# A queue model places TensorE's dependent steps, row maxima move within a unit's fill, long reciprocals go in quarters

## The chip, the cores and the metric

The kernel runs on one core of one Trainium2 chip. The metric is the device time of one execution in microseconds (us); the figure of a kernel is the median of its runs. Each engine of the core works through its own queue in order: TensorE (PE, with the weight loads as PEld), VectorE (DVE), ScalarE (ACT), GpSimd (POOL) and SyncE (SP), which issues the DMAs. An instruction that waits holds up everything behind it on its engine.

## The reference

Two layers (DEPTH 2) over 2048 frames of width 1024, in float32. A layer projects its input into four head groups of four heads each, with a SiLU gate per group, and ends in an output projection and a LayerNorm:

```python
ya = _banded_chunk_attention(aq, ak, av, A_PREV_CHUNKS, rel_bias=rel_bias)      # own chunk + 8 before
yb = _mla(bcq, bckv, bkr, positions, mla_q_norm, w_uq, mla_kv_norm, w_ukv)      # dense chunk-causal
yc = _banded_chunk_attention(qc, kc, cv, SWA_PREV_CHUNKS, sinks=swa_sinks)      # own chunk + 2 before
ym = _memory_attention(mq, mem, w_mem_kv)                                       # 256 memory tokens
gated = jnp.concatenate([ya * jax.nn.silu(ag), yb * jax.nn.silu(bg),
                         yc * jax.nn.silu(cg), ym * jax.nn.silu(mg)], axis=-1)
return _layer_norm(alpha * x + gated @ w_out, ln_gain, ln_bias)
```

All four are softmax attentions: scores, the row's maximum, exp, and the product with v. The kernel holds its operands as pairs (a rounded high part and the rest, `hi` and `lo`), so a product takes three matmuls.

## The kernel before, in words

A layer has three stages. The first computes groups C, M and A for four blocks of 512 frames, six units per block in the order C, M, A, C, M, A, each unit two heads. The second runs group B (`unit_b`, eight units of two heads, with growing numbers of keys). The third (`phase3`) is the output projection with the LayerNorm.

A unit hands `drive` two lists. Its *banks* are score tiles of 512 columns: `do_s` issues the score matmuls (`sc`) and two exps on ACT (`ph` and `p`, lines 478 and 480), `do_l` the difference `pl` on DVE or POOL (498), `do_pv` the product with v (`pv`). `do_s` runs two banks ahead of `do_pv` (LA = 2). Its *fill* is everything that must be done before its banks: projections (`pp`, eight steps of three matmuls), transposes of v (`put_v`: `vf` by ACT, then `pvt` on PE, 400), splits of q and k, and the *row maxima*. `drive` spreads the fill of unit j+1 over the banks of unit j in proportion to written costs; `final`, the fill of the third stage, goes over the last unit.

Row maxima (`maxes`): a matmul writes scores of 128 queries to a PSUM tile `mx` (there are two, shared with `pt`, `pst`, `ptr` and `ptab`), DVE reduces it into a column of `mcol` (449: an add and a maximum, with a read of the accumulator behind it; 880 in M and 1011 in B: a plain maximum). In C a `tensor_scalar` with the sink follows (725), in A and B a small reduction over key blocks (604, 1017). Then `max_row` transposes `mcol` on PE (`pt`, 440), ACT negates it into `mr` (442) and an SP DMA (443) writes the row under the queries, where the head's first `sc` matmul reads it.

The Tile framework sets the order on each engine from the order in which the code is written. The code defers steps with `Clock`: `now` counts TensorE time alone (columns over 2400 per us), and `later(dt, f)` runs `f` when that clock has passed `now + dt`. Before the change these delays are constants:

```python
        later(1.3, tr)       # put_v: pvt after vf
        later(1.0, f)        # max_row: pt after the last maximum
        later(1.2, stats)    # latent: pst after sf
        later(2.5, fin)      # latent_fin
```

If `do_s` reaches a head whose maximum row has not been emitted, `ck.until` emits deferred steps until it has.

Of the kernel before, what the change touches and what calls it, by code (L numbers as in the profile page):

```python
# [16 lines left out]
OP = mybir.AluOpType  # L17
# [76 lines left out]
class Clock:  # L94


    def __init__(self):
        self.now = 0.0
        self.heap = []
        self.n = 0  # L100

# [33 lines left out]
def hybrid(ctx, tc, x, mem, positions, w_in, rel_bias, q_norm, w_uq, kv_norm, w_ukv,  # L135
# [7 lines left out]
    act = nc.scalar.activation  # L143
    dma = nc.sync.dma_start
    tt = nc.vector.tensor_tensor
    stt = nc.vector.scalar_tensor_tensor
    ptt = nc.gpsimd.tensor_tensor
    ck = Clock()
    later = ck.later

# [242 lines left out]
    def put_v(p, vt, t0, n):  # L393
# [11 lines left out]
        later(1.3, tr)  # L405
# [19 lines left out]
    def gate_end(ge, dst):  # L425
# [4 lines left out]
        for z in range(4):  # L430
            def part(c=slice(128 * z, 128 * z + 128)):
                nc.vector.reciprocal(e[:, c], e[:, c])  # L432
                ptt(g[:, c], g[:, c], e[:, c], op=OP.mult)  # L433
# [3 lines left out]
    def max_row(mc, q2t, row, st, i):  # L437
# [119 lines left out]
    def unit_a(l, b, p, D):  # L557
# [24 lines left out]
        def maxes(i):  # L582
# [9 lines left out]
            def one(n):  # L592
                def f():
# [7 lines left out]
                    if n == len(pieces) - 1:  # L601
                        if b:
                            mc = mcol(4)
                            nc.vector.reduce_max(mc, st["mc2", i], axis=AX.X)
# [19 lines left out]
        fill += mix(rest, maxes(0) + maxes(1))  # L624
# [29 lines left out]
        return fill, banks  # L654
# [24 lines left out]
    def unit_c(l, b, p, D):  # L679
# [92 lines left out]
        return fill, banks  # L772

    def latent(l, b, k, p, D):
# [32 lines left out]
        later(1.2, stats)  # L807

    def latent_fin(l, b, D):
# [43 lines left out]
        later(2.5, fin)  # L853

    def unit_m(l, b, p, D):
# [10 lines left out]
        def maxes(i):  # L866
# [3 lines left out]
            def one(n):  # L870
                def f():
# [8 lines left out]
                    nc.vector.reduce_max(st["mc", i][:, 2 * n:2 * n + 2], m.rearrange("p (t k) -> p t k", t=2), axis=AX.X)  # L880
# [7 lines left out]
        fill += pg[:2] + mix(pg[2:], maxes(0) + maxes(1))  # L888
# [11 lines left out]
        return fill, banks  # L900
# [3 lines left out]
    def unit_b(l, b, p, D):  # L904
# [91 lines left out]
        def maxes(i):  # L996
# [3 lines left out]
            def one(n):  # L1000
                def f():
# [8 lines left out]
                    if j < b:  # L1010
                        nc.vector.reduce_max(acc, m, axis=AX.X)  # L1011
                    else:
                        ttr(m, mmask[:, 512 - w:512], acc)
                    if n == len(pieces) - 1:
                        if b:
                            mc = mcol(4)
                            nc.vector.reduce_max(mc, st["mc", i][:, :, 0:b + 1], axis=AX.X)
# [7 lines left out]
            + up([2], 128 * p, kdone) + up([2], 256 + 128 * p, lambda pv: put_v(pv, vpart(b), 0, 4)) \  # L1025
            + maxes(0) + maxes(1)
# [17 lines left out]
        return fill, banks  # L1044
# [6 lines left out]
    def drive(units, final):  # L1051
# [191 lines left out]
    def g_split(D, b, f):  # L1243
# [16 lines left out]
        return ld, sp  # L1260

    def g_prep(D, b):
        pr = [g_split(D, b, f) for f in range(8)]
        steps = []
        for f in range(8):
            def s(f=f):
# [203 lines left out]
```

## Time and profile before

| | us |
|---|---|
| median of 3 runs (lowest, highest) | 2663.76 (2657.4, 2665.67) |
| the profiled execution | 2667.25 |
| its span, first to last instruction | 2665.5 |
| PE busy | 2527.8 |
| DVE busy | 1877.9 |
| ACT busy | 1264.0 |
| POOL busy | 1070.4 |

PE is busy for 95% of the span, so 137.7 us are gaps in front of a matmul. A matmul's listed duration is its latency: neighbours overlap, and the pace is read from the distance between starts.

### The profile page before, as it was taken

The page shows a single profiled execution, that of the slowest core. Times are in us where ns is not written, and L with a number is a line of the kernel's source. Part 1 is how long each engine was busy: PE and PEld are TensorE (multiplying, and loading weights), DVE is VectorE, ACT ScalarE, POOL GpSimd, SP SyncE. Part 2 cuts the span into 40 slices and gives each one's busy share as a digit, 9 for nine tenths or more (in the row PEclk, how much of TensorE's full clock was granted, in tenths as well). Part 3 has the DMA queues.
Part 4 walks back from the last instruction along what each step waited for, and adds up shares of the span by engine and source line. Part 5 has one row for each costly group of instructions (what it writes and reads, how often), then busy time and mean ns, then how long its engine had stood idle before and what let it go on. Part 6 is the DMA issues. An engine that isn't in the chain of part 4 may idle for free.

```text
span 2665.5 us, 36469 instructions
## 1 busy us (share of the span) xinstructions
PE 2527.8 (95%) x12312; PEld 2080.7 (78%) x12312; DVE 1877.9 (70%) x3293; ACT 1264.0 (47%) x2255; POOL 1070.4 (40%) x835
## 2 busy tenths in 40 slices
PE   7899999998999899989999999999999999999998
PEld 6777777887878787768877788788788787877786
DVE  4767768658666876988766566566566578688786
ACT  4545455455444566650024444454544455767200
POOL 4343334343333344453343434434333433445343
PEclk9999999999999999989999999999999999999999
DMA  6545345345335423254345443443443454232432
GB/s 209 165 154 166 110 135 169 102 131 163 115 124 164 149 76 100 64 170 138 135 137 161 147 144 120 131 139 116 134 139 110 144 157 129 63 118 83 147 121 87
DMA packets 176443, 350.91 MB, mean 132 GB/s; under 512 B 25688, under 2 KB 48944, under 8 KB 176256
## 3 DMA queue, kind: packets, MB, share of 16 engines
q1 hardware_dynamic: 176256, 348.58, 42.0%
q8 instruction: 98, 1.61, 0.3%
q14 instruction: 89, 0.73, 0.1%
HBM read 247.43 MB, written 68.02 MB: 118 GB/s over the span
## 4 chain that ended last, share of the span: by engine, by line
PE 33%; DVE 9%; issue 8%; POOL 5%; ACT 3%; DMA 2%; SPq 0%; POOLq 0%; DVEq 0%; ACTq 0%
PE pp L305 15%; PE pv L305 6%; PE sc L305 5%; PE po L305 2%; PE mx L305 2%; DVE pl L498 1%; POOL xr L1344 1%; POOL xr L1343 1%; PE up L305 1%; POOL pl L498 1%; DVE mx L449 1%; DVE xr L1341 1%; ACT p L480 1%; DVE mcol L1011 1%; POOL rs L1337 1%
## 5 line engine op out<-in xcount | busy, mean ns | idle before, releaser
L293 POOL TENSOR_TENSOR wlo<-raw,whi 128x1024 fp32r<-128x1024 f32 x184 | 447.0, 2430 | 656.7 <-ACT whi L288 612.9
L305 PE MATMUL pp<-xh,whi 128*128 128x512 f32 x1472 | 593.6, 403 | 1.5 <-ACT e L415 1.4
L305 PE MATMUL pp<-xl,whi 128*128 128x512 f32 x1472 | 584.6, 397 | 2.5 <-DVE xl L353 1.3
L305 PE MATMUL pp<-xh,wlo 128*128 128x512 f32 x1472 | 583.7, 397 | 1.7 <-POOL wlo L293 1.7
L478 ACT ACTIVATE ph<-sc 128x512 fp32r<-128x512 f32 (+2 forms) x560 | 324.5, 580 | 422.5 <-PE sc L305 399.8
L305 PE MATMUL sc<-Y 96*128 96x512 f32 (+15 forms) x1840 | 466.3, 351 | 3.0 <-ACT p L480 1.5
L498 DVE TENSOR_TENSOR pl<-p,ph 128x512 fp32r<-128x512 f32 (+2 forms) x389 | 316.9, 817 | 186.5 <-ACT p L480 184.0
L305 PE MATMUL pv<-ph,Y 128*128 128x512 f32 (+3 forms) x1520 | 398.5, 343 | 7.9 <-DVE e L423 4.6
L288 ACT ACTIVATE whi<-raw 128x1024 fp32r<-128x1024 f32 x192 | 203.4, 1059 | 336.0 <-issue 131.9
L498 POOL TENSOR_TENSOR pl<-p,ph 128x512 fp32r<-128x512 f32 (+1 forms) x171 | 222.7, 1303 | 341.8 <-ACT p L480 268.8
L305 PEld LDWEIGHTS sc<-Y 96*128 96x128 f32 (+6 forms) x1840 | 317.7, 193 | 43.6 <-ACT p L480 2.9
L305 PEld LDWEIGHTS pp<-xh,wlo 128*128 128x128 f32 x1472 | 280.3, 190 | 63.1 <-POOL wlo L293 2.6
L305 PEld LDWEIGHTS pp<-xh,whi 128*128 128x128 f32 x1472 | 281.4, 191 | 57.5 <-ACT e L415 2.5
L480 ACT ACTIVATE p<-sc 128x512 f32<-128x512 f32 (+2 forms) x560 | 322.8, 576 | 3.1 <-POOL pl L498 3.0
L305 PEld LDWEIGHTS pp<-xl,whi 128*128 128x128 f32 x1472 | 281.1, 191 | 48.7 <-DVE xl L376 2.4
L305 PEld LDWEIGHTS pv<-ph,Y 128*128 128x128 f32 x1520 | 273.8, 193 | 46.1 <-issue 5.3
L305 PE MATMUL pv<-pl,Y 128*128 128x512 f32 (+3 forms) x760 | 265.6, 349 | 20.9 <-DVE pl L498 13.3
L305 PE MATMUL mx<-Y 128*128 128x256 f32 (+6 forms) x800 | 251.8, 340 | 19.5 <-DVE mcol L449 10.9
L449 DVE CUSTOM_DVE_ANT_0 mx<-mx,bts 128x128 f32<-128x128 f32 (+3 forms) x352 | 171.7, 494 | 78.9 <-PE mx L305 69.6
L305 PEld LDWEIGHTS mx<-Y 128*128 128x128 f32 (+1 forms) x800 | 151.8, 193 | 71.0 <-DVE mcol L449 24.3
L433 POOL TENSOR_TENSOR g<-g,e 128x128 f32<-128x128 f32 x192 | 116.1, 613 | 202.0 <-DVE e L432 188.7
L305 PEld LDWEIGHTS pv<-pl,Y 128*128 128x128 f32 x760 | 146.7, 193 | 50.4 <-DVE pl L498 23.6
(249 smaller groups left out, 3620.4 us busy)
## 6 DMA issues: line engine op xcount, KB each, us to landing
raw<-in_w_in_dram SPq DMA_DIRECT2D x184, 512.0 KB
Y<-Y SPq DMA_DIRECT2D x144, 128.0 KB
gr<-gT SPq DMA_DIRECT2D x64, 256.0 KB
gT<-g SPq DMA_DIRECT2D x48, 256.0 KB
cts<-sin SPq DMA_DIRECT2D x40, 256.0 KB
cts<-cos SPq DMA_DIRECT2D x40, 256.0 KB
xt<-in_xT_dram SPq DMA_DIRECT2D x32, 256.0 KB
raw<-in_w_out_dram SPq DMA_DIRECT2D x16, 512.0 KB
```

What stands on the lines that cost most here:

```text
L288: act(hi, raw, AF.Copy)
L293: ptt(lo, raw, f32(hi), op=OP.subtract)
L305: mm(o, lhs, rhs, start=start, stop=stop)
L433: ptt(g[:, c], g[:, c], e[:, c], op=OP.mult)
L449: nc.vector.tensor_tensor_reduce(m, m, table, op0=OP.add, op1=OP.max, scale=1.0, scalar=-3e38, accum_out=acc)
L478: act(bk["ph"][:, :width], sc[:, :width], AF.Exp, scale=scale)
L480: act(bk["p"][:, :width], sc[:, :width], AF.Exp, scale=scale)
L498: (ptt if on_pool else tt)(bk["pl"][:, :w], bk["p"][:, :w], f32(bk["ph"])[:, :w], op=OP.subtract)
L1011: nc.vector.reduce_max(acc, m, axis=AX.X)
L1337: ptt(rs, rs, mhalf[:, 0:1], op=OP.pow)
L1341: nc.vector.tensor_scalar(y[hf], y[hf], mv[:, 0:1], rs, op0=OP.subtract, op1=OP.mult)
L1343: eng(y[hf], y[hf], lgt[hf], op=OP.mult)
```

## The change: what it does, and the diff

`Clock` gets two tables: `free` (when each of DVE, ACT and POOL has finished what it was given) and `made` (when a tensor at an offset is written). Wrappers around the usual instructions (`act`, `tt`, `stt`, `ptt`, `rmax`, `recip`, `ttr`) enter a written cost. `after(ap, dt, f)` runs `f` when the clock has passed the moment at which `ap` is made plus `dt`. It replaces `later` for `pvt`, `pt` and `pst`; `latent_fin` waits 3.5 instead of 2.5. Not entered are `tensor_scalar`, `tensor_copy` and DMAs.

The row maxima move: in A and B the second head's become a third list, `late`, which `drive` spreads over the first half of the unit's own banks; in A the first head's are mixed into all but the last three projection steps; in C and M the last three or two projection steps stand behind all maxima; in B the first head's stand before the projection of v. The reciprocals over 128x512 for the third stage (1256) become four over 128x128, each a step of its own with a cost of 0.3.

```diff
 class Clock:
+    @staticmethod
+    def key(ap):
+        return ap.tensor.name, ap.offset
+
+    def use(self, eng, cost, out, *ins):
+        t = max([self.free.get(eng, 0.0), self.now] + [self.made.get(self.key(a), 0.0) for a in ins if hasattr(a, "tensor")])
+        self.free[eng] = t + cost
+        self.made[self.key(out)] = t + cost + 0.1
+
+    def ready(self, ap):
+        return max(self.now, self.made.get(self.key(ap), 0.0))
...
+    def tt(out, a, b, **kw):
+        ck.use("dve", 0.16 + 0.00115 * cols(out), out, a, b)
+        return nc.vector.tensor_tensor(out, a, b, **kw)
...
+    def after(ap, dt, fn):
+        later(ck.ready(ap) - ck.now + dt, fn)
...
-        later(1.3, tr)
+        after(vf, 0.1, tr)
...
-        later(1.0, f)
+        after(mc, 0.1, f)
...
     def ttr(m, table, acc):
+        ck.use("dve", 0.28 + 0.00108 * cols(m), acc, m)
...
-        fill += mix(rest, maxes(0) + maxes(1))
+        fill += mix(rest[:-3], maxes(0)) + rest[-3:]
+        late = maxes(1)
...
-        if p == 0:
-            fill = fill[:-2] + mix(fill[-2:], late)
-        else:
-            fill = fill[:-8] + mix(fill[-8:], late)
+        fill = fill[:-8] + mix(fill[-8:-3], late) + fill[-3:]
...
-        later(1.2, stats)
+        after(sf, 0.1, stats)
...
-        later(2.5, fin)
+        later(3.5, fin)
...
-        fill += pg[:2] + mix(pg[2:], maxes(0) + maxes(1))
+        fill += pg[:2] + mix(pg[2:6], maxes(0) + maxes(1)) + pg[6:]
...
-            + up([2], 128 * p, kdone) + up([2], 256 + 128 * p, lambda pv: put_v(pv, vpart(b), 0, 4)) \
-            + maxes(0) + maxes(1)
+            + up([2], 128 * p, kdone) + maxes(0) + up([2], 256 + 128 * p, lambda pv: put_v(pv, vpart(b), 0, 4))
+        late = maxes(1)
...
+        for j, u in enumerate(units):
+            if u[2]:
+                a = max(0, marks[j] - LA - 1)
+                jobs.append((a, max(a + 1, marks[j] + len(u[1]) // 2 - LA - 2), u[2]))
...
-        def sp():
+        def sp(z):
+            if f in (2, 3):
+                c = slice(128 * z, 128 * z + 128)
+                recip(st["d"][:, c], st["d"][:, c])
+                if z < 3:
+                    return
+                ptt(st["g"], st["g"], st["d"], op=OP.mult)
             hi, lo = gtile(b, f)
-            if f in (2, 3):
-                nc.vector.reciprocal(st["d"], st["d"])
-                ptt(st["g"], st["g"], st["d"], op=OP.mult)
...
-            steps.append((0.0, s))
+                steps.append((0.3, s))
```

Three places show how the order moves. The first is on PE, in the second M unit of the third block of layer 0: the end of its first head's maxima and their transpose `pt`. Before:

```order
L305 MATMUL mx<-Y 128x256 x2
L305 MATMUL pv<-ph,Y 128x128 x2
L305 MATMUL pv<-pl,Y 128x128
L305 MATMUL pv<-ph,Y 128x384 x2
L305 MATMUL pv<-pl,Y 128x384
L305 MATMUL sc<-Y 128x256 x4
L440 MATMUL pt<-identr,mcol 4x128
L305 MATMUL pp<-xh,whi_81 128x512
```

and now, where the same `pt` follows two steps of the next projection:

```order
L350 MATMUL pv<-ph,Y 128x256 x2
L350 MATMUL pv<-pl,Y 128x256
L350 MATMUL sc<-Y 128x256 x2
L350 MATMUL sc<-Y 128x128 x4
L350 MATMUL pp<-xh,whi_83 128x512
L350 MATMUL pp<-xl,whi_83 128x512
L350 MATMUL pp<-xh,wlo_84 128x512
L350 MATMUL pp<-xh,whi_83 128x512
L350 MATMUL pp<-xl,whi_83 128x512
L350 MATMUL pp<-xh,wlo_84 128x512
L485 MATMUL pt<-identr,mcol 4x128
L350 MATMUL pp<-xh,whi_83 128x512
```

Between the last `mx` pair of this head and its `pt` stood ten matmuls (five rows); now 32 rows stand there, of which the piece shows the last ten.

The second is on PE in layer 0's group B, at the transpose of the second head's maxima in the second unit of the second pair of heads. Before, that row is emitted while the previous unit still runs:

```order
L440 MATMUL pt<-identr,mcol 4x128
L305 MATMUL pv<-pl,Y 128x256
L305 MATMUL sc<-Y 128x512
L305 MATMUL pv<-ph,Y 128x512 x2
L305 MATMUL pv<-pl,Y 128x512
L305 MATMUL sc<-Y 128x512
L305 MATMUL up<-xh,whi_81 128x512 x3
L305 MATMUL up<-xh,wlo_82 128x512 x2
L305 MATMUL up<-xh,whi_83 128x512 x3
L305 MATMUL sc<-Y 128x512 x2
```

and now it is emitted inside its own unit, and the run of nine `sc` in the last row begins with the matmul that reads it:

```order
L485 MATMUL pt<-identr,mcol 4x128
L350 MATMUL pv<-ph,Y 128x128
L350 MATMUL pv<-pl,Y 128x128
L350 MATMUL mx<-Y 128x512
L350 MATMUL mx<-Y 128x256
L350 MATMUL pv<-ph,Y 128x256 x2
L350 MATMUL pv<-pl,Y 128x256
L350 MATMUL mx<-Y 128x512 x2
L350 MATMUL sc<-Y 128x512 x9
```

Between `pt` and that run stand nine matmuls of 2816 columns in all, where there were dozens.

The third is on DVE where the last banks of layer 0 run (`gd` are the operands of the long reciprocals, `pl` and `gm` belong to the banks, `Y<-raw` and `xl<-gr` to the third stage). Before:

```order
L1139 MEMSET bts_92 64x64
L498 TENSOR_TENSOR pl<-p,ph 128x512
L1256 RECIPROCAL gd<-gd 128x512
L1239 TENSOR_TENSOR Y<-raw_85,Y 128x512
L498 TENSOR_TENSOR pl<-p,ph 128x512 x2
L1256 RECIPROCAL gd<-gd 128x512
L498 TENSOR_TENSOR pl<-p,ph 128x512
L422 TENSOR_TENSOR gm<-pv,gm 64x512
L423 SCALAR_TENSOR_TENSOR gm<-gm,pv 64x512
```

and now:

```order
L190 RECIPROCAL gd<-gd 128x128
L174 TENSOR_TENSOR xl<-gr,xh 128x512
L174 TENSOR_TENSOR pl<-p,ph 128x512
L190 RECIPROCAL gd<-gd 128x128 x3
L174 TENSOR_TENSOR pl<-p,ph 128x512
L174 TENSOR_TENSOR Y<-raw_86,Y 128x512
L174 TENSOR_TENSOR pl<-p,ph 128x512
L190 RECIPROCAL gd<-gd 128x128 x2
L174 TENSOR_TENSOR pl<-p,ph 128x512
L190 RECIPROCAL gd<-gd 128x128 x2
```

Two reciprocals over 512 columns have become eight over 128, in groups of one to three between the `pl`.

## Rows read from the trace of the kernel before

**Rows 1.** The page, part 1: busy time and share of the span by engine

```profile
PE 2527.8 (95%) x12312; PEld 2080.7 (78%) x12312; DVE 1877.9 (70%) x3293; ACT 1264.0 (47%) x2255; POOL 1070.4 (40%) x835
```

**Rows 2.** Spans and granted clock

```profile
core 0: 2665.5 us, clock 0.980
```

**Rows 3.** Waits of PE over the span: total us, times, longest

```profile
PE pt L440 <- DVE mcol L880: 14.6, 12, 3.6
PE pv L305 <- DVE pl L498: 13.3, 14, 2.2
PE pvt L400 <- ACT vf L395: 12.3, 10, 4.1
PE pt L440 <- DVE mcol L725: 12.2, 6, 2.2
PE mx L305 <- DVE mcol L449: 10.9, 14, 2.0
...
PE pv L305 <- POOL pl L498: 7.2, 8, 2.0
...
PE pt L440 <- DVE mcol L604: 3.8, 4, 1.3
...
PE sc L305 <- DMA Y<-mr: 0.3, 1, 0.3
```

**Rows 4.** Busy time by stage: columns PE, PEld, DVE, ACT, POOL, clock, DMA

```profile
1190.00:1380.00 190.00, 188.31 (x846) 155.53 (x845) 146.33 (x194) 18.70 (x28) 75.50 (x68) 1.00 0.42 142
860.00:1190.00 330.00, 309.13 (x1433) 248.57 (x1432) 265.33 (x454) 212.61 (x416) 144.13 (x120) 0.96 0.37 111
```

**Rows 5.** Timeline of DVE at 600 us: start, duration, instruction

```profile
601.50 0.68 DVE L498 TENSOR_TENSOR pl<-p,ph 128x512 fp32r<-128x512 f32 x1
602.10 0.42 DVE L243 TENSOR_SCALAR kk<-kk 128x512 f32<-128x512 f32 x1
```

**Rows 6.** Timeline of PE at 600 us

```profile
604.20 0.63 PE L305 MATMUL pp<-xh,wlo 128*128 128x512 f32 x1
604.62 0.63 PE L305 MATMUL pp<-xh,whi 128*128 128x512 f32 x1
...
606.10 0.40 PE L305 MATMUL pp<-xh,whi 128*128 128x512 f32 x1
606.33 0.40 PE L305 MATMUL pp<-xl,whi 128*128 128x512 f32 x1
```

**Rows 7.** Timeline of all engines at 374 us

```profile
374.75 2.39 DVE L725 TENSOR_SCALAR mcol<-mcol,snk 128x4 f32<-128x4 f32 x1
374.77 2.34 POOL L293 TENSOR_TENSOR wlo<-raw,whi 128x1024 fp32r<-128x1024 f32 x1 [6.57 <-ACT whi L288]
```

**Rows 8.** Timeline of all engines at 1049 us

```profile
1049.23 0.41 PE L440 MATMUL pt<-identr,mcol 128*4 128x128 f32 x1
...
1051.81 0.47 PE L305 MATMUL sc<-Y 97*128 97x512 f32 x1 [0.29 <-DMA Y<-mr]
```

**Rows 9.** DVE groups by shape: busy us, mean ns, idle before

```profile
L432 DVE RECIPROCAL e<-e 128x128 f32<-128x128 f32 x192 | 174.6, 931 | 0.9
...
L1256 DVE RECIPROCAL gd<-gd 128x512 f32<-128x512 f32 x16 | 53.5, 3346 | 9.3 <-DMA gd<-gD 9.3
```

**Rows 10.** Line 725: durations in ns, min/median/max, first and last start

```profile
L725 DVE TENSOR_SCALAR mcol<-mcol,snk x32: 218/230/2389, 78.2 to 2096.9; 128x4 f32<-128x4 f32 x32
```

**Rows 11.** Waits of PE at the end of layer 0's banks, 1126 to 1187 us

```profile
PE pv L305 <- DVE pl L498: 6.8, 4, 2.2
PE pv L305 <- POOL pl L498: 2.3, 2, 2.0
```

**Rows 12.** Waits of PE at the end of layer 1's banks, 2350 to 2482 us

```profile
PE pv L305 <- POOL pl L498: 4.2, 3, 1.9
PE pv L305 <- DVE pl L498: 3.6, 4, 1.3
```

**Rows 13.** Waits of PE in the first 60 us

```profile
PE pvt L400 <- ACT vf L395: 6.0, 3, 4.1
```

More of the change, by code (lines that the diff above doesn't have):

```diff
@@ L100, in __init__ @@
         self.n = 0
+        self.free = {}
+        self.made = {}
+    @staticmethod
[7 more added lines that the diff above has]
+        return max(self.now, self.made.get(self.key(ap), 0.0))
     def later(self, dt, fn):
@@ L142, in hybrid, with cols, act, stt @@
     mm = nc.tensor.matmul
-    act = nc.scalar.activation
     dma = nc.sync.dma_start
-    tt = nc.vector.tensor_tensor
-    stt = nc.vector.scalar_tensor_tensor
-    ptt = nc.gpsimd.tensor_tensor
     ck = Clock()
     later = ck.later
+    def cols(ap):
+        n = 1
+        for d in ap.shape[1:]:
+            n *= d
+        return n
+    def act(out, a, fn, **kw):
+        ck.use("act", 0.17 + 0.00083 * cols(out), out, a)
+        return nc.scalar.activation(out, a, fn, **kw)
+    def tt(out, a, b, **kw):
+        ck.use("dve", 0.16 + 0.00115 * cols(out), out, a, b)
+        return nc.vector.tensor_tensor(out, a, b, **kw)
+    def stt(out, a, c, b, **kw):
+        ck.use("dve", 0.16 + 0.00115 * cols(out), out, a, b)
+        return nc.vector.scalar_tensor_tensor(out, a, c, b, **kw)
+    def ptt(out, a, b, **kw):
+        ck.use("pool", 0.1 + 0.0023 * cols(out), out, a, b)
+        return nc.gpsimd.tensor_tensor(out, a, b, **kw)
+    def rmax(out, a):
+        ck.use("dve", 0.14 + 0.00105 * cols(a), out, a)
+        return nc.vector.reduce_max(out, a, axis=AX.X)
+    def recip(out, a):
+        ck.use("dve", 0.1 + 0.0066 * cols(a), out, a)
+        return nc.vector.reciprocal(out, a)
+    def after(ap, dt, fn):
+        later(ck.ready(ap) - ck.now + dt, fn)
     sb = ctx.enter_context(tc.tile_pool(name="sb", bufs=1))
@@ L603, in f @@
                             mc = mcol(4)
-                            nc.vector.reduce_max(mc, st["mc2", i], axis=AX.X)
+                            rmax(mc, st["mc2", i])
                         else:
@@ L653, in unit_a @@
             banks += head_banks(hd, bl)
-        return fill, banks
+        return fill, banks, late
     def store_gate(pg, dst):
@@ L771, in unit_c @@
             banks += bl
-        return fill, banks
+        return fill, banks, []
     def latent(l, b, k, p, D):
@@ L899, in unit_m @@
             banks += head_banks(hd, bl)
-        return fill, banks
+        return fill, banks, []
     wide = [0]
@@ L1010, in f @@
                     if j < b:
-                        nc.vector.reduce_max(acc, m, axis=AX.X)
+                        rmax(acc, m)
                     else:
@@ L1043, in unit_b @@
             banks += head_banks(hd, bl, 96.0 ** -0.5, wide)
-        return fill, banks
+        return fill, banks, late
     def run_fill(fill):
@@ L1251, in ld @@
                 dma(st["d"], D["gD"][f - 2, b])
-        def sp():
+        def sp(z):
[5 more added lines that the diff above has]
+                ptt(st["g"], st["g"], st["d"], op=OP.mult)
             hi, lo = gtile(b, f)
-            if f in (2, 3):
-                nc.vector.reciprocal(st["d"], st["d"])
-                ptt(st["g"], st["g"], st["d"], op=OP.mult)
             act(hi, st["g"], AF.Copy)
             tt(lo, st["g"], f32(hi), op=OP.subtract)
-        return ld, sp
+        return ld, [lambda z=z: sp(z) for z in range(4 if f in (2, 3) else 1)]
     def g_prep(D, b):
@@ L1265, in g_prep, with s @@
         for f in range(8):
-            def s(f=f):
-                if f == 0:
-                    pr[0][0]()
-                    pr[1][0]()
-                if f + 2 < 8:
-                    pr[f + 2][0]()
-                pr[f][1]()
-            steps.append((0.0, s))
+            for j, sp in enumerate(pr[f][1]):
+                def s(f=f, j=j, sp=sp):
+                    if f == 0:
+                        pr[0][0]()
+                        pr[1][0]()
+                    if f + 2 < 8 and j == 0:
+                        pr[f + 2][0]()
+                    sp()
+                steps.append((0.3, s))
         return steps
```

10 lines of the change are left out of this document (5 added, 5 removed).

## The prediction

> **What bounds the kernel now.** I read the page first. TensorE is busy for 95% of a span of 2665.5 us [rows 1, 2], so it is the bound, and the only things to gain are its gaps, 2665.5 - 2527.8 = 137.7 us, and its clock: the granted clock is 0.980 on average [rows 2], a loss of 2% or 53 us. The stages come second. In the third stage PE is busy for 188.3 of 190 us at clock 1.00; in group B it is busy for 309.1 of 330 us at 0.96 [rows 4]. The gaps lie in the first two stages, where many small things feed PE.
>
> The view of who waited for whom then says what the gaps are [rows 3]. The transposes `pt` of the row maxima are the largest family: 14.6 us on M's reduction (line 880), 12.2 on C's `tensor_scalar` (725), 3.8 on A's (604). Then come `pv` on `pl` from DVE and POOL (13.3 + 7.2), `pvt` on `vf` (12.3) and `mx` on DVE (10.9). They add up to 74.3 us, over half of the gaps.
>
> The longest of M's, 3.6 us [rows 3], shows where a wait comes from and what it costs. It ended at 603.2 us. Between M's two reductions a `pl` and a `tensor_scalar` stood on DVE [rows 5], 0.68 + 0.42 us that the constant delay of 1.0 does not know. Afterwards the 512-column matmuls start 0.42 us apart (604.20 to 604.62), and two us later 0.23 us apart (606.10 to 606.33) [rows 6]: the lower of the two clock levels, 1.2 GHz, then the higher, 2.4. So a long gap is paid twice. On average it is 53/137.7 = 0.39 us of clock for each us of gap, and I take that for whatever goes or comes.
>
> **The change part by part.** No matmul is added or removed; 16 reciprocals become 64. So work on the bounding engine is the same, and the sum is about gaps.
>
> *The transposes of M.* That `pt` had ten matmuls behind its last maximum; now the last ten rows of 32 ahead of it are six of projection and four of the banks (first pair of pieces of the order). Counted over the order in the same way (distance of a `pt` from its last `mx`, 512 columns at 0.23 us), 22 of the 32 M heads had under 2.1 us, and 12 of them show a wait [rows 3]; now 10 have under 2.1, with 1.0 to 1.9. I keep 10/22 of 14.6 us and drop 8 us. Ends: nothing, since the entry used for M is the one of the first reduction (`made` is keyed by the row's offset, and the second reduction writes at offset 2), and all 14.6.
>
> *A's transposes.* The 24 of line 604 now have 2.7 us or more where most had 1.1 to 1.8: the 3.8 us go, and that is 4 in the sum. Ends 0 and 3.8.
>
> *C's transposes.* Here I count nothing. The key of `mcol` is its first column's, so the `pt` is placed by the first of four reductions, and the `tensor_scalar` behind the fourth is not entered at all. The distances stay at 0.9 to 1.4 us for most of the 32 heads. The long cases are no queue either: at 374.75 us the `tensor_scalar` on four elements took 2.39 us and ended with a POOL subtraction of 2.34 us that ran beside it [rows 7]; six such waits make up the 12.2 us. Of its 32 cases the median is 0.23 us and the longest 2.39 [rows 10]. The model cannot see this. Ends: all of the 12.2 us gone, or as much again.
>
> The Trainium skill has a rule for it, page "SBUF — State Buffer", section "Who interferes with whom": an operation of DVE in a two-port mode and one of GpSimd take a shared pair of ports for a whole instruction, and whoever comes second blocks fully. The trace agrees here (2.39 against 2.34 us, same end). By that rule a cost written for DVE alone is wrong whenever POOL is busy, and the change would come out as the second rival below has it, 2662.
>
> *`pvt` and `pst`.* 6.0 of the 12.3 us of `pvt` lie in the first 60 us [rows 13], where the transposes still follow their copy directly, and stay. Of the other 6.3 I drop 4, since the order gives over half of the `pvt` a longer distance. Ends 0 and 6.3. `pst` keeps its distance in 18 of 24 cases and is left at nothing.
>
> *Maxima spread out.* An `mx` tile can be written again only when DVE has read the one two before it. Counted as above, with the durations that the change writes for DVE, 64 places were too short by 20 us in sum; now 38 are, by 9 us. I drop 7 of 10.9 us. Ends 0 and 10.9.
>
> *Quartered reciprocals.* One took 3.346 us, during which no `pl` can pass, a quarter 0.931 us [rows 9]. The waits on `pl` where the third stage's preparation lies over the last banks are 6.8 + 2.3 us in layer 0 and 4.2 + 3.6 in layer 1 [rows 11, 12], 16.9 us. But the framework groups quarters again, up to three in a row (third pair of pieces), 2.8 us, and part of these waits is on POOL. What also helps is that most of the second block's subtractions now stand behind the last `pl`. I drop 9 us. Ends 0 and 16.9. The added 16 x (4 x 0.931 - 3.346) = 6 us of DVE are hidden: in the third stage DVE is busy for 146 of 190 us while PE hardly waits [rows 4]; if that cover were gone, 6 us.
>
> *The new wait.* A deferred `pt` pushes the row's DMA later, and the head's first `sc` needs that row. Before, this wait was 0.3 us in all [rows 3], and that one time shows the price: `pt` at 1049.23, and `sc` at 1051.81 after a wait of 0.29 [rows 8]. So a row needs 2.58 us from the start of `pt`. In group B the second head's maxima now lie in the unit's own first half; in the piece shown nine matmuls of 2816 columns, 2816/512 x 0.23 = 1.3 us, stand between. Counted over the 32 heads of group B, 9 are short by 1.1 to 1.7 us and 12 by 0.1 to 0.5, 15 us in sum (before: 4 heads, 2.7 us by the same count, 0.3 measured). Behind the waiting `sc` all of PE is queued, and behind that ACT's exps. I take 10 us, nearer the count than the tenth of it that the one measurement would give, since most are short by over 1 us. Ends 2 and 15.
>
> *Sum.* Gone 8 + 4 + 4 + 7 + 9 = 32 us of gaps, and 32 x 0.39 = 12 of clock; new 10 and 4. Net -30 us. The profiled execution took 2667.25 us, 3.5 over the median of 2663.76; so 2637 on its scale and **2633** on the median's. With every end at its better side the gaps gone are 14.6 + 3.8 + 12.2 + 6.3 + 10.9 + 16.9 = 64.7 against 2 new, -87 us with the clock: 2577. With every end at its worse side nothing goes and 15 + 12.2 + 6 come, +46: 2710.
>
> **The rivals.**
>
> *Late rows in group B (slower).* The price of 2.58 us holds if `pt` itself is on time. If DVE is behind its written costs there (`pl` and the maxima keep it busy for 265 of 330 us [rows 4]), `pt` waits too, and then each head pays the whole way from its reduction. 32 heads at 2.58 us are 83 us, 115 with the clock, against 44 gained: 2664 + 71 = 2735 in the extreme; it decides from 44/1.39/32 = 1.0 us a head on average, and 1.6 us a head would give 2691. For it: the short distances. Against: the one row measured cost 0.29 us though the count said it was short by more.
>
> *The waits move (no change).* DVE is next to bound in group B, and its blocks by POOL are not in the model. Half of the 32 `tensor_scalar` run free now (median 0.23 us [rows 10]). If the other half were blocked too, C's 12.2 us would double; and the 9 us of `pl`, some of which is on POOL [rows 11, 12], might not go. That is (12.2 + 9) x 1.39 = 29 us on the forecast: 2662. For it: nothing in the change keeps POOL away from DVE. Against: no part of it draws them together either.
>
> *More goes than counted (faster).* All but C's waits go, and the clock with them: 52.5 x 1.39 less 10 x 1.39 is -59 us: 2605. For it: a smoother DVE queue also ends the many gaps under 0.3 us. Against: M and C use the wrong entry.
>
> **How the numbers follow.** What can be told from no change is 0.3%, 8 us: faster means under 2655.8, slower over 2671.8. My forecast of 2615 to 2655 has 0.60, the faster rival 0.15, waits that move (2656 to 2672) 0.14, late rows 0.11. So faster 0.75, same 0.14, slower 0.11. The range leaves out the best end and most of the slower case: 2585 to 2670.
>
> **What would show it.** In the waits of PE after: `pt` on 880's kind at about 6 us, on A's near 0, on C's `tensor_scalar` still 8 to 16; `pvt` about 9, `mx` on DVE about 4; `pv` on `pl` over the last banks about 8; a new line, `sc` on the DMA of `mr`, with about 10 us in some 10 to 20 places, all in group B; the clock at 0.985 or so. The forecast is wrong if the clock stays at 0.980 with the gaps gone (then the 0.39 fails), if `pt` on C's `tensor_scalar` goes as well (then the lookup works better than its key), or if `sc` on `mr` exceeds 30 us.

## The result and the profile after

The changed kernel takes **2706.89 us** (median of 4 runs, 2700.73 to 2713.83) against 2663.74 of the kernel before: 1.0167 times as long, 95% interval 1.0136 to 1.0198. The forecast was 2633 (2585 to 2670): wrong, on the slower side.

The page of the changed kernel, part 1, answers to [rows 1], its span and clock to [rows 2]:

```profile
PE 2536.6 (94%) x12312; PEld 2082.6 (77%) x12312; DVE 1904.2 (70%) x3341; ACT 1252.6 (46%) x2251; POOL 1070.3 (40%) x835
```

```profile
core 0: 2703.3 us, clock 0.978
```

The gaps of PE are 2703.3 - 2536.6 = 166.7 us, 29.0 more than before; PE's busy time grew by 8.8 at a clock lower by 0.002. Read by stage, from the starts of the first `up` (group B begins) and the first `po` (the third stage begins) in the two timelines:

| stage | before, us | after, us | |
|---|---|---|---|
| start and first stage, layer 0 | 859 | 877 | +18 |
| group B, layer 0 | 317 | 329 | +12 |
| third stage, layer 0 (first to last `po`) | 187 | 187 | 0 |
| first stage, layer 1 | 799 | 804 | +5 |
| group B, layer 1 | 317 | 317 | 0 |
| third stage, layer 1 (first `po` to the end) | 186 | 189 | +3 |

The waits of PE over the whole span (total, times, longest) answer to [rows 3]. L186 is now the line of every plain maximum, L495 of the additions with a maximum, L178 of `stt`, L174 of `tt`:

```profile
PE mx L350 <- DVE Y L178: 33.2, 12, 4.3
PE pv L350 <- DVE pl L174: 16.1, 18, 2.4
PE pv L350 <- POOL pl L182: 12.4, 16, 3.4
PE sc L350 <- DMA Y<-mr: 9.8, 15, 1.1
...
PE pv L350 <- DVE e L178: 8.4, 3, 7.6
PE pp L350 <- DVE Y L174: 7.8, 3, 5.8
PE mx L350 <- DVE mcol L495: 7.6, 10, 1.5
PE pvt L445 <- ACT vf L170: 6.2, 3, 3.3
PE ptab L1175 <- DMA tr<-ext: 6.0, 1, 6.0
PE pt L485 <- DVE mcol L186: 5.8, 9, 1.5
...
PE pt L485 <- DVE mcol L495: 1.2, 3, 0.6
```

Four lines of the kernel before that the reader has not seen, same view:

```profile
PE pv L305 <- DVE e L423: 4.6, 1, 4.6
PE mx L305 <- DVE Y L385: 3.6, 3, 2.5
PE pp L305 <- DVE Y L376: 2.3, 2, 1.2
PE ptab L1127 <- DMA tr<-ext: 0.5, 1, 0.5
```

Most of what the change aimed at shrank: `pt` fell from 30.6 us [rows 3] to 7.0, `pvt` by 6.1, `mx` on its reductions by 3.3, 33 us together. `pv` on `pl`, the aim of the quarters, fell over the last banks from 16.9 us [rows 11, 12] to 8.8 (1147 to 1210 and 2384 to 2516 us), but rose over the whole span. And other lines grew by more: `mx` on the query's split +29.6, `sc` on the row's DMA +9.5, `pv` on `pl` +8.0, `pp` on `Y` +5.5, `ptab` on its transfer +5.5, `pv` on `e` +3.8.

The largest new line lies mostly in one place: the first `mx` of the **second M unit** of a block, right behind that unit's query projection (eight of its 12 waits, 24.1 of 33.2 us). One of them in layer 1, on DVE, POOL, ACT and PE (start, duration, instruction, idle time before it). The latent norm is the normalisation of group B's input, done in the first stage: `cr` is the latent read back from DRAM, `rb` its row of scales, `lh` and `ll` are the high and the low part of the result. `Y<-pp` are the two heads' query splits:

```profile
1929.83 1.13 DVE L178 SCALAR_TENSOR_TENSOR ll<-cr,gn,lh 64x512 fp32r<-64x512 f32 x1 [3.48 <-ACT whi L170]
1930.88 2.82 DVE L174 TENSOR_TENSOR pl<-p,ph 128x512 fp32r<-128x512 f32 x1
1933.73 0.68 DVE L178 SCALAR_TENSOR_TENSOR Y<-pp,Y 64x512 fp32r<-64x512 f32 x1
1935.08 0.69 DVE L178 SCALAR_TENSOR_TENSOR Y<-pp,Y 64x512 fp32r<-64x512 f32 x1 [0.66 <-ACT Y L170]
```

```profile
1929.12 1.29 POOL L182 TENSOR_TENSOR cr<-cr,rb 128x512 f32<-128x512 f32 x1 [3.33 <-DMA rb<-rst]
1930.38 2.79 POOL L182 TENSOR_TENSOR wlo<-raw,whi 128x1024 fp32r<-128x1024 f32 x1
```

```profile
1929.66 0.58 ACT L170 ACTIVATE Y<-pp 64x512 fp32r<-64x512 f32 x1
1932.20 0.72 ACT L170 ACTIVATE lh<-cr,gn 128x512 fp32r<-128x512 f32 x1 [1.95 <-DMA lhl<-lh]
1934.45 0.59 ACT L170 ACTIVATE Y<-pp 64x512 fp32r<-64x512 f32 x1 [1.53 <-DVE Y L178]
```

```profile
1934.47 0.79 PE L350 MATMUL mx<-Y 128*128 128x256 f32 x2 [3.59 <-DVE Y L178]
1935.07 0.63 PE L350 MATMUL pp<-xh,whi 128*128 128x512 f32 x1
1935.49 0.63 PE L350 MATMUL pp<-xl,whi 128*128 128x512 f32 x1
```

DVE stood idle for 3.48 us at the head of its queue with `ll`, then `pl` took 2.82 us beside a POOL subtraction of 2.79 (the median of all `pl` on DVE is 0.69), and only then came the split that PE waited for. So some 2.1 of PE's 3.59 us were spent in that long `pl`. A `pl` of 2.82 or 2.83 us stands directly ahead of the split in the four longest of the eight waits (396, 826, 1934 and 2147 us), each time beside a POOL subtraction that follows POOL's own step of the norm, `cr`, which had waited 2.70 to 3.65 us for its transfer. Over the span 51 of the 359 `pl` of 512 columns on DVE take over 1.5 us, against 21 before. ACT too stood idle, 1.95 us, with `lh`, which waits for a store of the norm's part before, and the second head's copy stood behind it. Afterwards the matmuls start 0.42 us apart, the lower clock level, as in [rows 6].

### The profile page after: what moved, and what is told of

Read it like the earlier page. It is cut to its first block, busy times and chain, and to the rows that moved or that the text cites. A ratio compares the mean times of both kernels' runs of the same rounds, so it can differ in the third digit from the quotient of the medians.

```text
span 2703.3 us, 36652 instructions
## 1 busy us (share of the span) xinstructions
PE 2536.6 (94%) x12312; PEld 2082.6 (77%) x12312; DVE 1904.2 (70%) x3341; ACT 1252.6 (46%) x2251; POOL 1070.3 (40%) x835
## 5 line engine op out<-in xcount | busy, mean ns | idle before, releaser
L182 POOL TENSOR_TENSOR wlo<-raw,whi 128x1024 fp32r<-128x1024 f32 (+1 forms) x192 | 459.9, 2396 | 646.1 <-ACT whi L170 578.5
L174 DVE TENSOR_TENSOR pl<-p,ph 128x512 fp32r<-128x512 f32 (+2 forms) x389 | 360.4, 928 | 168.6 <-ACT p L170 157.5
L350 PE MATMUL sc<-Y 96*128 96x512 f32 (+17 forms) x1840 | 454.8, 351 | 19.0 <-DMA Y<-mr 9.8
L350 PEld LDWEIGHTS sc<-Y 96*128 96x128 f32 (+6 forms) x1840 | 319.4, 194 | 72.0 <-DMA Y<-mr 11.7
L350 PE MATMUL pv<-pl,Y 128*128 128x512 f32 (+3 forms) x760 | 266.6, 351 | 29.2 <-DVE pl L174 16.1
L350 PE MATMUL mx<-Y 128*128 128x256 f32 (+6 forms) x800 | 244.8, 344 | 46.4 <-DVE Y L178 33.2
L495 DVE CUSTOM_DVE_ANT_0 mx<-mx,bts 128x128 f32<-128x128 f32 (+3 forms) x352 | 171.1, 499 | 112.0 <-PE mx L350 107.5
L186 DVE TENSOR_REDUCE mcol<-mx 128x1 f32<-128x512 f32 (+1 forms) x256 | 173.1, 681 | 32.2 <-PE mx L350 29.4
```

What stands on the lines that cost most here:

```text
L174: return nc.vector.tensor_tensor(out, a, b, **kw)
L182: return nc.gpsimd.tensor_tensor(out, a, b, **kw)
L186: return nc.vector.reduce_max(out, a, axis=AX.X)
L350: mm(o, lhs, rhs, start=start, stop=stop)
```

## Experiments

Times are medians; each ratio is to the runs of the kernel before that were taken on the same chip, with its 95% interval. "Before +" is the kernel before with one part of the change, "after +" the changed kernel with one edit.

| run | | us | ratio |
|---|---|---|---|
| quarters_only | before + reciprocals in quarters | 2662.39 | 1.0005 [0.9993, 1.0017] |
| model_only | before + the model for `pvt`, `pt`, `pst` | 2682.75 | 1.0070 [1.0048, 1.0092] |
| row_model | before + the model for `pt` alone | 2676.85 | 1.0059 [1.0040, 1.0078] |
| row_pull | row_model and the model for `pst`, rows taken out alone | 2682.92 | 1.0079 [1.0055, 1.0102] |
| row_cap | row_model, deferral up to 2.5 | 2672.39 | 1.0030 [1.0016, 1.0044] |
| fills_only | before + all moved maxima | 2691.74 | 1.0108 [1.0091, 1.0125] |
| m_fill_only | before + M's maxima moved | 2664.01 | 1.0009 [0.9995, 1.0022] |
| c_fill_only | before + C's maxima moved | 2664.97 | 1.0017 [1.0004, 1.0030] |
| late_only | before + the late lists of A and B | 2683.01 | 1.0085 [1.0069, 1.0102] |
| late_A | before + A's late lists | 2666.05 | 1.0022 [1.0007, 1.0037] |
| m_between | quarters, `pst`, M's maxima in between | 2667.26 | 1.0021 [1.0009, 1.0032] |
| latent_in_place | after + norm without one wait | 2697.21 | 1.0130 [1.0112, 1.0148] |
| no_gate_recip_before | before less 192 reciprocals | 2666.70 | 1.0024 [1.0012, 1.0035] |
| no_gate_recip_after | after less 192 reciprocals | 2691.96 | 1.0136 [1.0109, 1.0163] |
| latent_early | c_fill_only + norm closer together | 2663.77 | 1.0005 [0.9995, 1.0015] |
| latent_late | c_fill_only + norm 14 later | 2658.34 | 0.9989 [0.9977, 1.0001] |
| latent_far | c_fill_only + norm 36 later | 2640.86 | 0.9930 [0.9914, 0.9945] |
| far_grouped | latent_far + two edits | 2632.01 | 0.9896 [0.9881, 0.9910] |

The ratios in us of 2662: quarters +1, model +19, fills +29; M's part of the fills is +2, C's +5, the late lists' +23 (A +6, so B some +17). The three parts sum to 49 against 44 for the whole, so they add, within the intervals; what is left over, -4, holds `latent_fin`'s 3.5, which was not run by itself.

**The three parts.**

```
quarters_only   -  recip(gd 128x512)            + 4 x recip(gd 128x128), each a fill step
model_only      -  later(1.3, tr) / later(1.0, f) / later(1.2, stats)
                +  after(vf, 0.1, tr) / after(mc, 0.1, f) / after(sf, 0.1, stats)
fills_only      the fills and late lists of the change; the delays as before
```

> The kernel before with one part of the change: the reciprocals of the third phase's gate preparation (L1256, 3346 ns each) cut in quarters. Theory A (the quarters are sound, the loss of the whole change lies elsewhere): the gaps they caused in PE go, 2652 to 2660 us, some 5 to 12 us under the kernel before. Theory B (the quarters themselves put more work in the way of the last attention units): 2664 us or more, and the stretch from 1040 to 1190 us loses time on PE.

> The kernel before with the queue model alone: put_v, max_row and stats place their PE step by the modelled end of what they read; the fills, late lists, the final latent step's delay (2.5) and the long reciprocals are those of before. Theory A (the loss comes from where the maxima stand in M's fill, with the latent norm at the head of VectorE's queue): the waits of the transposes go and nothing else comes, 2640 to 2660 us. Theory B (the deferral itself costs: a step that waits for a row of maxima empties the list of deferred steps early, rope sums and loads among them): 2680 to 2700 us, with new waits where the rope sums come early.

> The kernel before with the moved fills alone: maxima of M and C nearer to their query's split, second maxima of A and B in the late lists; delays fixed as before (1.3, 1.0, 1.2, 2.5), long reciprocals whole. Theory A (where the maxima stand makes the loss): 2690 to 2710 us, with stalls of 2.5 to 4.5 us at the first mx of each second M unit. Theory B (the deferral itself costs): 2655 to 2670 us.

The quarters gain nothing. At the end of layer 0's banks [rows 11] `pv` waits for `pl` no less:

```profile
PE pv L305 <- DVE pl L498: 7.4, 6, 2.3
PE pv L305 <- POOL pl L498: 4.1, 4, 1.9
```

11.5 us against 9.1, in more and shorter pieces, and 9.6 against 7.8 in layer 1 [rows 12]. Model and fills each cost; both theories were half right.

**The fills one by one.**

```
m_fill_only   - fill += pg[:2] + mix(pg[2:], maxes(0) + maxes(1))
              + fill += pg[:2] + mix(pg[2:6], maxes(0) + maxes(1)) + pg[6:]
m_between     + fill += pg[:3] + mix(pg[3:7], maxes(0) + maxes(1)) + pg[7:]   (with quarters and pst)
c_fill_only   - fill[:-2] + mix(fill[-2:], late)   (p == 0; the last 8 for p == 1)
              + fill[:-8] + mix(fill[-8:-3], late) + fill[-3:]
late_only     A: mix(rest[:-3], maxes(0)) + rest[-3:]; B: maxes(0) ahead of v; late = maxes(1)
late_A        the same in A alone
```

> The kernel before with one line of the change: M's four steps of maxima stand behind steps 3, 4, 5 and 6 of the gate's projection instead of 4, 5, 7 and 8. Theory F1 (M's fill alone makes the loss of the moved fills: mx reaches the query's split before VectorE has made it): 2680 to 2692 us, with waits of mx for the split of 25 to 40 us in all against 3.6. Theory F2 (C's fill or the late lists of A and B make it): 2658 to 2670 us.

> The kernel before with the quarters, stats by the model, and M's maxima behind steps 4, 5, 6 and 7: the first as far behind the query's split as before, the last one step (0.65 us) further from the scores. If the first mx is what counts, mx waits no more than before (about 4 us) and the transposes in M wait some 0.6 us less each: 2652 to 2660 us. If VectorE's queue at that place is full anyway, the maxima one step closer together wait as in the changed kernel's M: 2666 to 2680 us.

> The kernel before with one edit: C's maxima of the first pair mixed over five steps of the fill's last eight, as in the change. Theory C1 (C's fill makes the loss of the moved fills: the transpose that held TensorE up for 2.4 us behind VectorE's locked tensor_scalar is met earlier, and TensorE then reaches the next M unit's maxima before VectorE has made their query): the waits for mcol L725 (12.2 us) fall under 3 us and those of mx for the split rise to 20 us or more, 2675 to 2692 us. Theory C2 (the loss is in the late lists of A and B): 2650 to 2664 us.

> The kernel before with the late lists alone: the second head's maxima of A and B stand in the first half of their own unit's banks. Theory C1 (C's fill makes the loss): 2655 to 2668 us. Theory C2 (the late lists make it, by VectorE's burst behind the query of the A units): 2680 to 2692 us, with mx for Y of 4 us at the first late maxima of each A unit.

> The late lists in the A units alone; B as in the kernel before. If the A units make the loss (their maxima now run among the scores of their own first head, and M's fill behind them comes early): 2675 to 2684 us. If the B units make it: 2655 to 2667 us.

M's fill is innocent by itself, against F1, and it does not help either: its `pt` wait 14.5 us, 14.6 before. M's in-between version is no better. C's fill costs 5 us, not the 13 to 30 of C1, but it is the run that teaches most. Its waits of PE:

```profile
PE mx L305 <- ACT p L480: 26.8, 7, 6.2
PE mx L305 <- DVE Y L385: 16.1, 7, 3.7
...
PE pt L440 <- DVE mcol L877: 5.8, 7, 1.9
PE pt L440 <- DVE mcol L604: 3.8, 4, 1.2
PE mx L305 <- DVE mcol L449: 3.0, 4, 1.2
...
PE pt L440 <- DVE mcol L725: 0.4, 1, 0.4
```

These `pt` and `mx`-on-reduction lines were 14.6 + 3.8 + 10.9 + 12.2 = 41.5 us in [rows 3] and are 13.0 here: 28.5 us gone, C's blocked `tensor_scalar` (725) among them. The first two lines were 1.4 and 3.6 and are 42.9: 37.9 us come, most of them at the first `mx` of the second M units (5.87, 6.17 and 4.36 us in layer 0). One of them, on ACT, DVE and PE:

```profile
391.39 0.72 ACT L841 ACTIVATE lh<-cr,gn 128x512 fp32r<-128x512 f32 x1 [1.78 <-DMA lhl<-lh]
...
392.86 0.68 DVE L385 SCALAR_TENSOR_TENSOR Y<-pp,Y 64x512 fp32r<-64x512 f32 x1
...
394.69 0.59 ACT L480 ACTIVATE p<-sc 128x512 f32<-128x512 f32 x1
...
395.33 0.79 PE L305 MATMUL mx<-Y 128*128 128x256 f32 x2 [5.87 <-ACT p L480]
```

This `mx` starts 0.05 us after ACT's `p` ends and 1.79 us after the DVE half of its own split: in this kernel what it meets is `p`, which stands behind `lh` and the second head's copy on ACT. Why it is made to wait for `p`, which it does not read, is not shown. The stalls only moved one dependency on.

The late lists are where time is really lost, and mostly in B. Waits of PE in group B of layer 0, late_only (867 to 1186 us):

```profile
PE pt L485 <- DVE mcol L186: 3.2, 7, 1.3
PE pt L485 <- DVE mcol L495: 2.0, 2, 1.6
PE sc L350 <- DVE gm L178: 1.5, 1, 1.5
PE sc L350 <- DMA Y<-mr: 1.2, 1, 1.2
```

In late_A all `pt` together wait 0.8 us there; in layer 1's group B it is 5.8 us against 0.2. The second head's reductions now stand on DVE among the `pl` of the first head; that this makes the transposes late is my reading, and no run tests it. The norm is not what costs here: over the span `mx` waits 6.4 us on DVE's `Y`, 4.3 before. Part of the 17 us is not seen in these lines and stays open.

**The model for the rows.**

```
row_model   - later(1.0, f)         + after(mc, 0.1, f)        (pvt and pst as before)
row_pull    + a head that lacks its row takes only deferred rows from the list; `now` stays;
              + after(sf, 0.1, stats), as in the whole model
row_cap     + later(min(ready(mc) - now + 0.1, 2.5), f)
```

> The kernel before with the queue model in max_row alone; put_v, stats, fills and reciprocals as before. Theory D1 (the deferred rows make the model's loss of 20 us: a head whose row is still deferred pops the other deferred steps early): 2675 to 2685 us, with the waits for DVE Y, DVE e and xl that the whole model showed. Theory D2 (the loss comes from put_v's deferral of the values' transposes): 2655 to 2665 us.

> As row_model, with one more edit: a head whose row is still deferred takes only the deferred rows out of the list, and leaves every other deferred step and the planner's clock where they are. Theory P1 (the popping of the other steps is the loss): the waits of the transposes stay small and the new ones go, 2645 to 2662 us. Theory P2 (the loss lies in the rows themselves, which now come just ahead of the scores that read them, and in what VectorE does when the transposes no longer hold TensorE up): 2672 to 2685 us.

> As row_model (the kernel before with max_row placed by the model), but the deferral is at most 2.5 on the planner's clock. Theory R1 (the far deferrals in the MLA stage are the model's loss): its loss in the first layer's MLA stage (13 us in row_model) goes, 2655 to 2666 us. Theory R2 (the short deferrals in C, M and A cost as much as they save, and the loss is spread): 2670 to 2680 us.

D1 holds: the rows make 16 of the model's 19 us. Its length sits in group B of layer 0, 329 us from the first `up` to the first `po` against 317 (layer 1: 318 against 317). There the modelled queue runs ahead of the planner's clock, rows are deferred until their head calls for them, and the call moves that clock on by up to 15 and can pop another step. By the planner's own clock the same happens in layer 1, which loses 1 us; why layer 0 alone pays stays open. P1 falls: popping the rows alone is no better (`sc` on the row's DMA 7.1 us against 0.9 in row_model), though that run also places `pst` by the model. The cap brings group B back to 315 us in its profile, but the whole stays 8 us above before by the ratio: R1 for the place, not for the whole. What the short deferrals cost elsewhere stays open. A model for `pvt` or `pst` without one for the rows was not tried: nothing would then make sure that a transposed v is written ahead of its reader.

**Is VectorE's load the pace?**

```
no_gate_recip_before, no_gate_recip_after   - recip(e[:, c], e[:, c])   in gate_end
```

> The kernel before without the 192 reciprocals of the gates (L432, 931 ns each, 174.6 us of VectorE in all), so the output is not the reference's. Theory V1 (in the stretch after each latent VectorE's burst is the pace, and a transpose that waits is only the place where TensorE meets it): the transposes' waits in M fall to a third, 2610 to 2640 us. Theory V2 (the waits come from the order of instructions, not from the amount of VectorE's work): above 2645 us.

> The changed kernel without the same 192 reciprocals. Theory V1 (the change only moved the place where TensorE meets VectorE's burst): with the burst smaller the distance between the two kernels falls from 43 us to under 15. Theory V2 (the changed kernel's new waits come from its order alone, the latent norm and the steps popped early among them): the distance stays above 30 us.

V1 falls for the kernel before: DVE's busy time fell from 1877.9 to 1731.5 us, and it gained nothing. The distance between the two kernels shrank from 43 to 25 us by the medians, 30 by the ratios, between the theories; the changed kernel's own gain (1.0136 against 1.0167) lies within the two intervals. So the amount of DVE's work is not the pace of the kernel before; that the order of its queue is, the next runs have to show.

**The latent norm in the way.** Its three parts read a latent and a row of scales back from DRAM, POOL multiplies, ACT makes `lh`, DVE `ll`, and both are stored; each of these waits at the head of its engine's queue.

```
latent_in_place   - stt(lo, cr, g, hi)               + stt(cr, cr, g, hi)
latent_early      - later(4.0 + 5.0 * k, norm)       + later(4.0 + 3.0 * k, norm), low part in place
latent_late       + later(18.0 + 5.0 * k, norm)
latent_far        + later(40.0 + 8.0 * k, norm)      - later(2.2, fin2)   + later(4.0, fin2)
far_grouped       latent_far; M: act, act, stt, stt instead of act, stt, act, stt;
                  rope angles: later(4.0, ...) behind the load of the positions
```

> The changed kernel with one edit: the latent norm writes its low part in place into cr, so that VectorE's instruction no longer waits for a free lt buffer, that is for the transfer that stores the part before. Nothing else in the order is meant to move. Theory A1 (the latent norm's wait at the head of VectorE's queue makes the stalls of the second M units): those eight stalls of 1 to 4.5 us shrink below 1.5 us each, VectorE's idle time before this instruction goes from 30 to about 10 us, and the kernel takes 2670 to 2685 us. Theory A2 (the maxima simply stand too near to the split, whatever else is queued): the stalls stay above 2 us, 2698 to 2707 us.

> The kernel before with C's fill of the change, and the latent norm out of the way: its three parts 3.0 apart instead of 5.0, with the low part written in place so that no part waits for the store of the one before; all three then stand ahead of the second M unit's query split on VectorE. Theory H1 (the norm's instructions, waiting for transfers at the heads of the queues, are what mx waits for there): the first mx of the second M units wait under 2 us each instead of 4 to 6, the kernel takes 2635 to 2652 us. Theory H2 (the query's split is late there whatever stands beside it): 2660 us or more, with these waits as in c_fill_only.

> As latent_early, the other way: the norm's parts start 14 later on the planner's clock, so that the second and third stand behind the second M unit's query split (the first still ahead of it). Theory H1: the first mx of the second M units wait under 2.5 us each, but the maxima's reductions behind the split may now meet the norm: 2640 to 2658 us. Theory H2: 2660 us or more.

> The kernel before with C's fill of the change, and the latent norm's three parts started 40 later on the planner's clock and 8 apart (4 and 5 before), with 4.0 instead of 2.2 between its loads and its first use. No part then stands within six instructions ahead of a unit's query copy on ScalarE (22 did). Theory H1 (the norm is what these mx wait for): the first mx of the second M units in the second layer, where no rope angles are made, wait under 2.5 us each against 1.9 to 3.9 in c_fill_only and 3.4 to 5.1 in latent_early; ScalarE's idle time before lh nearly goes; 2640 to 2656 us. Theory H2 (the split itself is late, its two halves one behind the other on ScalarE and VectorE): these waits stay above 3 us, 2657 to 2666 us.

> As latent_far, and two more edits: M's split issues both heads' copies on ScalarE before both subtractions on VectorE (one head behind the other before), and the rope angles of the next block are issued 4.0 behind the load of their positions, so that their first cast does not wait for it at the head of VectorE's queue. Theory H1 with these two as the rest of the wait: the first mx of the second M units wait under 1.5 us each in both layers, 2630 to 2648 us. If the waits only move on once more (to the maxima's reductions, or to the late maxima of A): 2650 to 2662 us, with as much idle time of TensorE in another group.

Groups of instructions (busy, mean ns | idle before, what ended it): ACT's `lh` and PE's `mx` of 256 columns. Before, then after, then c_fill_only, latent_early and latent_far:

```profile
L844 ACT ACTIVATE lh<-cr,gn 128x512 fp32r<-128x512 f32 (+1 forms) x24 | 17.3, 722 | 10.4 <-POOL cr L838 6.6 <-DMA lhl<-lh 2.4 <-DVE ll L845 1.2
L305 PE MATMUL mx<-Y 128*128 128x256 f32 x304 | 80.9, 305 | 16.1 <-DVE mcol L449 10.9 <-DVE Y L385 3.6 <-ACT p L480 1.4
```

```profile
L170 ACT ACTIVATE lh<-cr,gn 128x512 fp32r<-128x512 f32 (+1 forms) x24 | 17.4, 723 | 28.5 <-DMA lhl<-lh 14.7 <-POOL cr L182 13.6
L350 PE MATMUL mx<-Y 128*128 128x256 f32 x304 | 84.8, 319 | 37.8 <-DVE Y L178 29.5 <-DVE mcol L495 7.4 <-issue 0.5
```

```profile
L841 ACT ACTIVATE lh<-cr,gn 128x512 fp32r<-128x512 f32 (+1 forms) x24 | 17.4, 724 | 38.2 <-DMA lhl<-lh 18.6 <-POOL cr L835 17.1 <-DVE Y L385 2.4
L305 PE MATMUL mx<-Y 128*128 128x256 f32 x304 | 83.6, 315 | 39.1 <-ACT p L480 26.8 <-DVE Y L385 7.9 <-DVE mcol L449 3.0
```

```profile
L840 ACT ACTIVATE lh<-cr,gn 128x512 fp32r<-128x512 f32 (+1 forms) x24 | 17.3, 723 | 39.6 <-POOL cr L835 39.6
L305 PE MATMUL mx<-Y 128*128 128x256 f32 x304 | 83.7, 315 | 44.9 <-ACT p L480 37.1 <-DVE Y L385 3.3 <-DVE mcol L449 3.1
```

```profile
L841 ACT ACTIVATE lh<-cr,gn 128x512 fp32r<-128x512 f32 (+1 forms) x24 | 17.3, 722 | 43.0 <-POOL cr L835 43.0
L305 PE MATMUL mx<-Y 128*128 128x256 f32 x304 | 81.1, 305 | 12.5 <-ACT p L480 4.6 <-DVE Y L385 4.0 <-DVE mcol L449 2.3
```

In the changed kernel and in c_fill_only, PE no longer stalls on its transposes, reaches the norm sooner, and finds its transfers still on the way: ACT's idle time before `lh` goes from 10.4 to 28.5 and 38.2 us, and PE's before `mx` from 16.1 to 37.8 and 39.1. latent_in_place takes one of the norm's waits away and gains 10 us, less than half of what A1 asked, at overlapping intervals; the stalls stay, as A2 had it (`mx` on the split 30.4 us against 33.2, DVE's idle time before the low part 28.7 against 30.8). latent_early comes out as H2 forecast, at 2663.77 us with first `mx` of second M units that wait 1.9 to 6.5 us. At the spot the last part now waits for POOL's `cr` on ACT shortly ahead of the query's copies, and DVE's split for the first head ends at 1899.70:

```profile
1895.86 0.72 ACT L840 ACTIVATE lh<-cr,gn 128x512 fp32r<-128x512 f32 x1 [3.26 <-POOL cr L835]
...
1898.39 0.58 ACT L384 ACTIVATE Y<-pp 64x512 fp32r<-64x512 f32 x1
...
1899.01 0.69 DVE L385 SCALAR_TENSOR_TENSOR Y<-pp,Y 64x512 fp32r<-64x512 f32 x1 [0.72 <-ACT Y L384]
...
1899.73 0.59 ACT L384 ACTIVATE Y<-pp 64x512 fp32r<-64x512 f32 x1 [0.75 <-DVE Y L385]
```

latent_late, with the norm 14 later, fits neither theory: 2658.34 us, and five of the eight first `mx` still wait 2.5 us or more.

latent_far moves all three parts behind the splits of the units that follow, and settles it for C's fill: 23 us less than c_fill_only on its own scale (0.9930 against 1.0017), no first `mx` of a second M unit in layer 1 that waits over 0.3 us, and C's transposes free as well. One expectation was wrong: ACT's idle time before `lh` is 43.0 us, more than ever. It is the same wait in a place where nothing behind it is needed soon.

far_grouped beats both kernels, 0.9896 [0.9881, 0.9910]: 27 us under before, 72 under the changed kernel. Its two edits were not run apart, so which one gives the last 9 us is open. The expected waits under 1.5 us hold in layer 1; in layer 0 two first `mx` still wait 2.0 and 2.9 us. Two runs are missing: the norm moved without C's fill, which may be worth as much by itself, and the norm moved in the changed kernel.

## Why the prediction was wrong

**The step that failed** is the one that turned stalls into time: "Gone 8 + 4 + 4 + 7 + 9 = 32 us of gaps". I priced each wait that goes and not the next reader of the same queues. In c_fill_only 28.5 us of waits go, 37.9 come, and the time is up by 5. Whether PE waits 2.4 us at C's transpose or reaches the second M unit 2.4 us earlier is the same while ACT, DVE and POOL have a step of the norm at the head of their queues that waits for a transfer; with the norm moved, latent_far gets 23 us back. I did not look at this DRAM round trip, although it stood in the trace of before with 10.4 us. My rival "the waits move" (2662) had the kind of thing right and named POOL's blocks. That is a part of it in the changed kernel, some 2.1 us in four of the eight stalls, and its "no part of it draws them together either" was wrong: 51 long `pl` against 21.

**The costs were the larger error.** I had one new cost, 10 us of gaps. Run by themselves the late lists cost 23 us and the rows' model 16, most of the 44, and not by the norm: `mx` waits on DVE's `Y` 6.4 us in late_only and 8.4 in row_model, 34.6 in the changed kernel. What makes these two costs is seen only in part.

**By terms.** M's transposes: 8 us forecast to go; all of M's, A's and B's plain reductions together now wait 5.8, so they went, but not by M's fill (14.5 us left in m_fill_only); C's fill or the rows' model bring these lines down. A's are in the same line; A's late lists cost 6. C's: I left them at nothing because their entry in the model is the wrong one, and the model by itself does leave 10.8 us of them (model_only). My sign took their going for a lookup that works; it is C's fill that frees them (0.4 us in c_fill_only), a part of the change that I had read only for DVE's distances. `pvt`: 4 forecast, 6.1 gone. `mx` on its reductions: 7 forecast, 3.3 gone, for a spreading whose late lists cost 23. Quarters: 9 forecast; over the last banks 8.1 went in the changed kernel, but the quarters by themselves leave more there than before and measure 1.0005. The new wait on the row's DMA: 10 forecast, 9.8 in 15 places, by luck: I put all of it in group B, where 2.2 + 1.3 us of it are. Never priced: `latent_fin` from 2.5 to 3.5, the deferred steps that a missing row pops early, and rows deferred far in group B, which lost 12 us in layer 0.

**The slower rival** named group B and late rows. B of layer 0 did lose 12 us, and in late_only the transposes of B are late as it said, but not by 32 heads that each pay 2.58; it had no term for the first stage, which lost 23 of the 38 us. The clock's 0.39 us per us of gap came out again as an average: 0.022 x 2703.3 = 59 us against 166.7 of gaps, 0.36. As a price for gaps that go or come it is no constant (last section).

## What to carry to other kernels

A wait in the profile is where a follower meets what is ahead of it; before counting it as gain, follow the same engines' queues to the next instruction that the follower needs, and find there what waits for a transfer at a queue's head. Such a round trip through DRAM belongs where nothing behind it in the queue is needed soon, however long it then waits: 43 us of it in the right place cost 23 us less than 38 us of it in the wrong one. A planner that defers steps needs a latest time for each, and should be tried part by part: of three parts here none gained, and the gain lay in a thing outside the change, into which one of them, C's fill, ran.

## What the runs showed of the hardware

With 146 us less work on DVE (8% of its busy time) the kernel before took 1.0024 of its time: VectorE, busy for 70% of the span, was not its bound by the amount of work.

ACT's copy of the second head's query starts 0.03 to 0.04 us after DVE's subtraction for the first head ends, in the cases shown (1934.41 to 1934.45; 1899.70 to 1899.73), though it reads other partitions of the same PSUM tile. The Trainium skill, page "PSUM — Partial Sum Buffer", section "PSUM bank collisions raise a hardware error", says that engines collide only in the same bank and the same group of 32 partitions; by that the wait would be the framework's and not the chip's. No run here shows the two side by side; far_grouped only puts both copies first.

In far_grouped more than one us was gained for each us of gap taken away: it has 2630.2 - 2511.4 = 118.8 us of gaps against 137.7, 18.9 less, and a span shorter by 35.3 at clock 0.986:

```profile
PE 2511.4 (95%) x12312; PEld 2062.5 (78%) x12312; DVE 1862.9 (71%) x3293; ACT 1258.9 (48%) x2251; POOL 1070.1 (41%) x835
```

That is 1.9 us per us, more than the 1.39 with which I worked. It is no fixed rate: late_only has 157.0 us of gaps, 19.3 more than before, in a span longer by 10.8 at clock 0.982, and no_gate_recip_before 149.4, 11.7 more, in a span shorter by 3.4 at clock 0.985.
